# RMSNorm over 16,384 rows of 512: the order of the transfers, and the scaling spread over three engines

## The chip, the cores and the metric

The kernel runs on one core of a Trainium2 chip. The metric is the device time of one execution in microseconds (us); lower is better.

## The reference

```python
def reference(x, gamma):          # x: 16 x 1024 x 512 float32, gamma: 512 float32
    eps = 1e-5
    rms = np.sqrt(np.mean(x ** 2, axis=-1, keepdims=True) + eps)
    return (x / rms * gamma).astype(np.float32)
```

Each row of 512 numbers is divided by its own root mean square and multiplied, column by column, by `gamma`. 33.55 MB are read and as many written.

## The kernel before

The 16,384 rows are cut into four tiles (t = 0 to 3). A tile has 32 rows in each of the 128 partitions, so a partition's share of it is one run of 64 KB in the input, in SBUF and in the output. Three buffers, `slots[0]` to `slots[2]`, hold a tile each; the fourth tile goes into slot 0 again, once the first tile is stored (`slot_of`).

The computation is in place and goes by groups of 8 rows per partition. `row_stats` (L63) finds the rows' sums of squares in one of two ways, by turns. In one, ScalarE squares one row at a time and accumulates its sum itself (L76). In the other, ScalarE squares four rows into PSUM (L70) and VectorE sums them (L71). ScalarE then takes the root (L82) and VectorE the reciprocal, `rstd` (L83). `apply` (L86) multiplies each row by its `rstd` and by `gamma_b` (gamma copied to every partition) in one VectorE instruction (L88). The statistics of the next group are written ahead of the scaling of this one; Tile's scheduler sets the final order on each engine.

All large transfers are issued by the engine SP, on one queue, in the order of the program. `load` is L42, `store` L45. An instruction on SP that must wait holds up those behind it. Tile 0 comes in two loads; the others are issued by `transfers` (L100) after the group that they are tied to:

```python
if (t, g) == (0, 0):
    store(0, 0, 0, 1); load(1, 1, 0, 32); load(2, 2, 0, 16)
    store(0, 0, 1, 2); load(2, 2, 16, 32)
elif (t, g) == (0, 24): store(0, 0, 2, 32)
elif (t, g) == (1, 8):
    store(1, 1, 0, 16); load(3, 0, 0, 16); load(3, 0, 16, 32)
elif (t, g) == (1, 24): store(1, 1, 16, 32)
elif (t, g) == (2, 24): store(2, 2, 0, 32)
elif (t, g) == (3, 8):  store(3, 0, 0, 16)
elif (t, g) == (3, 24): store(3, 0, 16, 32)
```

The arguments are tile, slot, first row and row after the last. Below is the function with the line numbers that the profile uses.

Of the kernel before, what the change touches and what calls it, by code (L numbers as in the profile page):

```python
# [1 line left out]

# [4 lines left out]


@with_exitstack
def kernel(  # L10
    ctx: ExitStack,
    tc: tile.TileContext,
    x: bass.AP,
    gamma: bass.AP,
    out: bass.AP,
):
    nc = tc.nc
    P = nc.NUM_PARTITIONS
    eps = 1e-5
    fp32 = mybir.dt.float32  # L20
    AF = mybir.ActivationFunctionType
    OP = mybir.AluOpType

    xf = x.flatten_outer_dims()
    of = out.flatten_outer_dims()
    N, D = xf.shape
    R = 32
    G = 8
    H = 4
    assert N == 4 * P * R  # L30

    xv = xf.rearrange("(t p r) d -> t p r d", p=P, r=R)
    ov = of.rearrange("(t p r) d -> t p r d", p=P, r=R)

    const = ctx.enter_context(tc.tile_pool(name="const", bufs=1))
    stats = ctx.enter_context(tc.tile_pool(name="stats", bufs=4))
    psum = ctx.enter_context(tc.tile_pool(name="psum", bufs=2, space=bass.MemoryType.PSUM))

    slots = [const.tile([P, R, D], fp32, name=f"slot{i}") for i in range(3)]

    def load(t, slot, r0, r1):
        nc.sync.dma_start(out=slots[slot][:, r0:r1], in_=xv[t][:, r0:r1])  # L42

    def store(t, slot, r0, r1):
        nc.sync.dma_start(out=ov[t][:, r0:r1], in_=slots[slot][:, r0:r1])  # L45

    load(0, 0, 0, 8)
    load(0, 0, 8, 32)

    gamma_row = const.tile([1, D], fp32)  # L50
    nc.scalar.dma_start(out=gamma_row, in_=gamma.unsqueeze(0))
    ones_col = const.tile([1, P], fp32)
    nc.vector.memset(ones_col, 1.0)  # L53
    gamma_psum = psum.tile([P, H, D], fp32, name="sq")
    nc.tensor.matmul(gamma_psum[:, 0], ones_col, gamma_row, start=True, stop=True)  # L55
    gamma_b = const.tile([P, D], fp32)
    nc.vector.tensor_copy(out=gamma_b, in_=gamma_psum[:, 0])  # L57

    eps_t = const.tile([P, 1], fp32)
    nc.vector.memset(eps_t, eps)  # L60
    sq_scratch = const.tile([P, D], fp32)

    def row_stats(slot, g):  # L63
        ss = stats.tile([P, G], fp32, name="ss")
        rms = stats.tile([P, G], fp32, name="rms")
        rstd = stats.tile([P, G], fp32, name="rstd")
        if (g // G) % 2:
            for h in range(0, G, H):
                sq = psum.tile([P, H, D], fp32, name="sq")
                nc.scalar.activation(out=sq, in_=slots[slot][:, g + h : g + h + H, :], func=AF.Square)  # L70
                nc.vector.tensor_reduce(  # L71
                    out=ss[:, h : h + H], in_=sq, axis=mybir.AxisListType.X, op=OP.add
                )
        else:
            for r in range(G):
                nc.scalar.activation(  # L76
                    out=sq_scratch,
                    in_=slots[slot][:, g + r, :],
                    func=AF.Square,
                    accum_out=ss[:, r : r + 1],  # L80
                )
        nc.scalar.activation(out=rms, in_=ss, func=AF.Sqrt, bias=eps_t, scale=1.0 / D)  # L82
        nc.vector.reciprocal(out=rstd, in_=rms)  # L83
        return rstd

    def apply(slot, g, rstd):  # L86
        for r in range(G):
            nc.vector.scalar_tensor_tensor(  # L88
                out=slots[slot][:, g + r, :],
                in0=slots[slot][:, g + r, :],  # L90
                scalar=rstd[:, r : r + 1],
                in1=gamma_b,
                op0=OP.mult,
                op1=OP.mult,
            )

    groups = [(t, g) for t in range(4) for g in range(0, R, G)]
    slot_of = [0, 1, 2, 0]

    def transfers(t, g):  # L100
        if (t, g) == (0, 0):
            store(0, 0, 0, 1)
            load(1, 1, 0, 32)
            load(2, 2, 0, 16)
            store(0, 0, 1, 2)
            load(2, 2, 16, 32)
        elif (t, g) == (0, 24):
            store(0, 0, 2, 32)
        elif (t, g) == (1, 8):
            store(1, 1, 0, 16)  # L110
            load(3, 0, 0, 16)
            load(3, 0, 16, 32)
        elif (t, g) == (1, 24):
            store(1, 1, 16, 32)
        elif (t, g) == (2, 24):
            store(2, 2, 0, 32)
        elif (t, g) == (3, 8):
            store(3, 0, 0, 16)
        elif (t, g) == (3, 24):
            store(3, 0, 16, 32)  # L120

    ahead = row_stats(0, 0)
    for k, (t, g) in enumerate(groups):
        rstd = ahead
        if k + 1 < len(groups):
            tn, gn = groups[k + 1]
            ahead = row_stats(slot_of[tn], gn)
        apply(slot_of[t], g, rstd)
        transfers(t, g)


# [1 line left out]
_INS = ['x', 'gamma']  # L133
_OUTS = [((16, 1024, 512), 'float32')]


# [23 lines left out]
```

## Time and profile before

| | |
|---|---|
| median of 14 runs | 162.2 us (161.78 to 163.03) |
| profiled execution | 161.77 us |
| its span | 160.0 us |
| VectorE (DVE) busy | 122.6 us, 77% |
| ScalarE (ACT) busy | 80.1 us, 50% |
| GpSimd (POOL) busy | 0.2 us |
| moved | 67.13 MB, mean 420 GB/s |

A row of groups names line, engine, operation, output and inputs with their shapes and count; after the first bar stand the busy time in us and the mean ns of one instruction, after the second the engine's idle time just before these instructions and what ended it. In the row of DMA slices each digit is the busy share of a fortieth of the span in tenths. A row of waits names who waited for whom, the total in us, how many times, and the longest. "DMA" is the group of 16 transfer engines, "SPq" the queue that issues on SP.

### The profile page before, as it was taken

How to read it: one execution, taken by the hardware profiler on the slowest of the kernel's cores; microseconds unless marked ns; L12 is line 12 of the kernel's file. 1: busy time of each engine (PE TensorE's matmuls, PEld its weight loads, DVE VectorE, ACT ScalarE, POOL GpSimd, SP SyncE). 2: the span in 40 equal slices, each digit the busy share in tenths (PEclk: the TensorE clock that was granted, in tenths of full speed). 3: DMA queues.
4: the chain of work that ended last, by engine and by line, in shares of the span. 5: the costliest groups of instructions: out<-in, count | busy, mean ns of one | idle time of the engine just before them, and what ended most of it. 6: DMA issues, size and time to landing. Idle time of an engine off the chain costs nothing.

```text
span 160.0 us, 409 instructions
## 1 busy us (share of the span) xinstructions
PE 2.0 (1%) x2; PEld 0.5 (0%) x2; DVE 122.6 (77%) x163; ACT 80.1 (50%) x162; POOL 0.2 (0%) x4
## 2 busy tenths in 40 slices
PE   4000000000000000000000000000000000000000
PEld 1000000000000000000000000000000000000000
DVE  0101928999999509999999999999999999996000
ACT  3098029991291999996900960069709950000000
POOL 0000000000000000000000000000000000000000
DMA  5999999699699999997999999999997996999993
GB/s 197 524 393 393 406 512 524 262 524 492 295 395 400 452 500 401 494 476 338 415 393 475 434 401 451 451 410 426 467 516 311 508 492 295 467 434 410 451 442 156
DMA packets 2164, 67.13 MB, mean 420 GB/s; under 512 B 241, under 2 KB 241, under 8 KB 498
## 3 DMA queue, kind: packets, MB, share of 16 engines
q1 hardware_dynamic: 2160, 67.11, 97.8%
q14 instruction: 2, 0.02, 0.0%
q10 hardware_dynamic: 2, 0.00, 0.0%
HBM read 33.56 MB, written 33.55 MB: 419 GB/s over the span
## 4 chain that ended last, share of the span: by engine, by line
DVE 67%; DMA 14%; ACT 7%; issue 2%; DVEq 0%; SPq 0%
DVE slot L88 48%; DVE ss L71 18%; DMA slot<-in_x_dram 14%; ACT sq_scratch L76 3%; ACT sq L70 3%; DVE rstd L83 1%; ACT rms L82 1%; DVEq L155 0%; SPq L42 0%
## 5 line engine op out<-in xcount | busy, mean ns | idle before, releaser
L88 DVE SCALAR_TENSOR_TENSOR slot<-slot,rstd,gamma_b 128x512 f32<-128x512 f32 x128 | 85.8, 741 | 0.1
L76 ACT ACTIVATE sq_scratch<-slot 128x512 f32<-128x512 f32 x64 | 40.0, 625 | 9.9 <-DMA slot<-in_x_dram 8.6
L70 ACT ACTIVATE sq<-slot 128x2048 f32<-128x2048 f32 x16 | 29.8, 1865 | 18.9 <-DVE ss L71 11.5
L71 DVE TENSOR_REDUCE ss<-sq 128x4 f32<-128x2048 f32 x16 | 35.9, 2277 | 3.6 <-ACT sq L70 3.6
L82 ACT ACTIVATE rms<-ss,eps_t 128x8 f32<-128x8 f32 x16 | 4.6, 297 | 26.2 <-DVE ss L71 26.0
L83 DVE RECIPROCAL rstd<-rms 128x8 f32<-128x8 f32 x16 | 3.1, 196 | 16.2 <-ACT rms L82 16.2
L76 ACT ACTIVATION_READ_ACCUMULATOR sq_scratch<-slot 128x1 f32 x64 | 11.9, 187 | 0.0
L57 DVE COPY gamma_b<-sq 128x512 f32<-128x512 f32 x1 | 0.7, 692 | 3.2 <-PE sq L55 3.2
L55 PE MATMUL sq<-gamma_row,ones_col 1*128 1x512 f32 x2 | 2.0, 1122 | 2.1 <-DMA gamma_row<-in_gamma_dram 2.1
L76 ACT ACT_TABLE_LOAD x1 | 1.3, 1283 | 1.3 <-PEq L144 1.3
L82 ACT ACT_TABLE_LOAD x1 | 1.3, 1283 | 0.0
L53 DVE MEMSET ones_col<- 1x128 f32 x1 | 0.2, 165 | 0.8 <-PEq L144 0.8
L55 PEld LDWEIGHTS sq<-gamma_row,ones_col 1*128 1x128 f32 x2 | 0.5, 308 | 2.1 <-issue 2.1
L144 POOL MEMSET const-bfloat16-1.0<- 128x1 bf16 x1 | 0.1, 101 | 0.0
L144 POOL MEMSET const-uint8-127<- 128x1 uint8 x1 | 0.1, 101 | 0.0
L144 POOL MEMSET const-float32-0.0<- 128x1 f32 x1 | 0.1, 98 | 0.2 <-issue 0.2
L144 POOL MEMSET const-float32-1.0<- 128x1 f32 x1 | 0.1, 98 | 0.0
L60 DVE MEMSET eps_t<- 128x1 f32 x1 | 0.1, 59 | 0.0
## 6 DMA issues: line engine op xcount, KB each, us to landing
slot<-in_x_dram SPq DMA_DIRECT2D x4, 4096.0 KB, 32.1
out_dram<-slot SPq DMA_DIRECT2D x4, 4096.0 KB, 18.3
out_dram<-slot SPq DMA_DIRECT2D x1, 7680.0 KB
slot<-in_x_dram SPq DMA_DIRECT2D x1, 6144.0 KB, 21.7
slot<-in_x_dram SPq DMA_DIRECT2D x1, 2048.0 KB, 7.1
out_dram<-slot SPq DMA_DIRECT2D x2, 256.0 KB, 21.3
gamma_row<-in_gamma_dram ACTq DMA_DIRECT2D x1, 2.0 KB
slot<-in_x_dram SPq DMA_DIRECT2D x1, 25.9
```

The lines of the kernel that those rows point to most:

```text
L53: nc.vector.memset(ones_col, 1.0)
L55: nc.tensor.matmul(gamma_psum[:, 0], ones_col, gamma_row, start=True, stop=True)
L57: nc.vector.tensor_copy(out=gamma_b, in_=gamma_psum[:, 0])
L60: nc.vector.memset(eps_t, eps)
L70: nc.scalar.activation(out=sq, in_=slots[slot][:, g + h : g + h + H, :], func=AF.Square)
L71: nc.vector.tensor_reduce(out=ss[:, h : h + H], in_=sq, axis=mybir.AxisListType.X, op=OP.add)
L76: nc.scalar.activation(out=sq_scratch, in_=slots[slot][:, g + r, :], func=AF.Square, accum_out=ss[:, r : r + 1],)
L82: nc.scalar.activation(out=rms, in_=ss, func=AF.Sqrt, bias=eps_t, scale=1.0 / D)
L83: nc.vector.reciprocal(out=rstd, in_=rms)
L88: nc.vector.scalar_tensor_tensor(out=slots[slot][:, g + r, :], in0=slots[slot][:, g + r, :], scalar=rstd[:, r : r + 1], in1=gamma_b, op0=O ...
L144: nc = _bacc.Bacc("TRN2", target_bir_lowering=False, num_devices=1)
```

## The change

The transfers are in another order. The first tile comes in three loads, the second tile's load is issued ahead of the first store, and the last tile's two loads stand between the first tile's store and the second tile's. That store is one transfer of 64 KB rows. The engine order is now the program's own (`manual_schedule`).

The groups have 8 rows twice and then 16 rows. All sums of squares go the second way: ScalarE squares 7, 5 and 4 rows (4 and 4 in the small groups) into PSUM or SBUF by turns, VectorE sums them. Of each group's rows, the last 3, 7 or 8 (the last number of a group's entry) are scaled on GpSimd, in two instructions: by `rstd`, then by gamma. The others are scaled by `rstd` one row at a time on ScalarE and by gamma in bulk on VectorE, in halves where the group has 16 rows. `declare_no_dep` takes from the bulk multiply those waits for transfers and GpSimd work on the same rows that ScalarE has had already. Gamma is fetched in six pieces, and its copy to all partitions is made by ScalarE.

```diff
     load(0, 0, 0, 8)
-    load(0, 0, 8, 32)
+    load(0, 0, 8, 16)
+    load(0, 0, 16, 32)
+    load(1, 1, 0, 32)
...
+    groups = [
+        (0, 0, 8, (4, 4), 3),
+        (0, 8, 8, (4, 4), 3),
+        (0, 16, 16, (7, 5, 4), 7),
+        (1, 0, 16, (7, 5, 4), 8),
+        (1, 16, 16, (7, 5, 4), 8),
+        (2, 0, 16, (7, 5, 4), 8),
+        (2, 16, 16, (7, 5, 4), 7),
+        (3, 0, 16, (7, 5, 4), 7),
+        (3, 16, 16, (7, 5, 4), 3),
+    ]
...
+    def square_sums(ss, t, g, r, m, k):
+        home, name, most = ((psum, "sq_psum", 7), (const, "sq_sbuf", 5))[k % 2]
+        sq = home.tile([P, most, D], fp32, name=name)
+        rows = slots[slot_of[t]][:, g + r : g + r + m, :]
+        nc.scalar.activation(out=sq[:, :m], in_=rows, func=AF.Square)
+        nc.vector.tensor_reduce(
+            out=ss[:, r : r + m, 0], in_=sq[:, :m], axis=mybir.AxisListType.X, op=OP.add
+        )
...
+    def scale_by_pool(rstd, t, g, n, share):
+        part = slots[slot_of[t]][:, g + n - share : g + n, :]
+        by_row = rstd[:, n - share : n].to_broadcast([P, share, D])
+        nc.gpsimd.tensor_tensor(out=part, in0=part, in1=by_row, op=OP.mult)
+        last = nc.gpsimd.tensor_tensor(
+            out=part, in0=part, in1=gamma_b.to_broadcast([P, share, D]), op=OP.mult
+        )
...
+    def scale_rows(rstd, t, g, r0, r1):
+        x = slots[slot_of[t]]
+        for r in range(r0, r1):
+            nc.scalar.activation(out=x[:, g + r, :], in_=x[:, g + r, :], func=AF.Copy, scale=rstd[:, r])
+        part = x[:, g + r0 : g + r1, :]
+        scaled = nc.vector.tensor_tensor(out=part, in0=part, in1=gamma_b.to_broadcast([P, r1 - r0, D]), op=OP.mult)
+        for slot, b0, b1, earlier in before_scale:
+            if slot == slot_of[t] and b0 < g + r1 and g + r0 < b1:
+                tc.declare_no_dep(scaled.ins, earlier.ins, reason="ScalarE waited for it before it scaled these rows")
 
     def transfers(t, g):
         if (t, g) == (0, 0):
             store(0, 0, 0, 1)
-            load(1, 1, 0, 32)
             load(2, 2, 0, 16)
             store(0, 0, 1, 2)
-            load(2, 2, 16, 32)
-        elif (t, g) == (0, 24):
-            store(0, 0, 2, 32)
-        elif (t, g) == (1, 8):
-            store(1, 1, 0, 16)
+            load(2, 2, 16, 24)
+            store(0, 0, 2, 3)
+            load(2, 2, 24, 32)
+        elif (t, g) == (0, 16):
+            store(0, 0, 3, 16)
+            store(0, 0, 16, 32)
             load(3, 0, 0, 16)
             load(3, 0, 16, 32)
-        elif (t, g) == (1, 24):
-            store(1, 1, 16, 32)
-        elif (t, g) == (2, 24):
+        elif (t, g) == (1, 16):
+            store(1, 1, 0, 32)
+        elif (t, g) == (2, 16):
             store(2, 2, 0, 32)
-        elif (t, g) == (3, 8):
+        elif (t, g) == (3, 0):
             store(3, 0, 0, 16)
-        elif (t, g) == (3, 24):
+        elif (t, g) == (3, 16):
             store(3, 0, 16, 32)
...
+    for k, group in enumerate(groups):
+        t, g, n, pieces, share = group
+        mine = n - share
+        half = (mine + 1) // 2
+        ahead = groups[k + 1 :][:1]
+        ss, todo = pieces_of(ahead[0]) if ahead else (None, [])
+        scale_by_pool(rstd, t, g, n, share)
+        for piece in todo[:2]:
+            square_sums(*piece)
+        if n < 16:
+            scale_rows(rstd, t, g, 0, mine)
+        else:
+            scale_rows(rstd, t, g, 0, half)
+        for piece in todo[2:]:
+            square_sums(*piece)
+        if n == 16:
+            scale_rows(rstd, t, g, half, mine)
         transfers(t, g)
+        for nxt in ahead:
+            rstd = inverse_rms(ss, nxt[2])
```

## The prediction, made before the changed kernel ran

> **What bounds the kernel now.** I read the page's row of DMA slices and its queue table first, because reading and writing 32 MiB each way is most of the work; then the groups, then the waits of the queue SP, then VectorE's timeline round the one store that comes nearest to being late.
>
> ```profile
> DMA  5999999699699999997999999999997996999993
> ...
> q1 hardware_dynamic: 2160, 67.11, 97.8%
> ```
>
> The transfer engines are full from the second slice to the last but one, and SP's queue fills 97.8% of their span. The trace's packet records say the same without rounding: the first load packet starts 1.74 us into the span, the last store packet ends at 158.8, and no engine of the 16 is without a packet between. A 64 KB packet took 2.418 us; a tile (32 rows of 2 KB in each of 128 partitions) is 8 such packets per engine, **19.34 us**. Eight tile transfers (four in, four out) are 154.8 of the 157.1 us. So the compute engines matter only where a store comes too late to keep the stream going.
>
> ```profile
> L88 DVE SCALAR_TENSOR_TENSOR slot<-slot,rstd,gamma_b 128x512 f32<-128x512 f32 x128 | 85.8, 741 | 0.1
> L76 ACT ACTIVATE sq_scratch<-slot 128x512 f32<-128x512 f32 x64 | 40.0, 625 | 9.9 <-DMA slot<-in_x_dram 8.6
> L70 ACT ACTIVATE sq<-slot 128x2048 f32<-128x2048 f32 x16 | 29.8, 1865 | 18.9 <-DVE ss L71 11.5
> L71 DVE TENSOR_REDUCE ss<-sq 128x4 f32<-128x2048 f32 x16 | 35.9, 2277 | 3.6 <-ACT sq L70 3.6
> ```
>
> These are the prices: 741 ns to scale a row, 625 for a row's ScalarE pass, 1865 for squares and 2277 for sums of four rows. GpSimd has none of the work. The queue's own waits:
>
> ```profile
> SPq L45 <- DVE slot L88: 120.5, 7, 29.8
> SPq L155 <- DMA out_dram<-slot: 12.0, 2, 9.6
> SPq L45 <- DMA slot<-in_x_dram: 10.3, 2, 6.3
> SPq L42 <- DMA out_dram<-slot: 8.4, 1, 8.4
> ```
>
> SP stands 120.5 us behind VectorE, and it costs nothing: each store is issued while earlier transfers still run. How near it comes is seen on VectorE:
>
> ```profile
> 105.94 9.97 DVE L88 SCALAR_TENSOR_TENSOR slot<-slot,rstd,gamma_b 128x512 f32<-128x512 f32 x15
> 115.84 4.48 DVE L71 TENSOR_REDUCE ss<-sq 128x4 f32<-128x2048 f32 x2
> ```
>
> The 15 rows end tile 2 at 115.9; the packet records show the sixth tile transfer done at **119.1**, and tile 2's store is the seventh. The cover is 3.2 us, of which about 1.0 is issue (the first load is issued at 0.73 and its first packet starts at 1.74).
>
> **What the Trainium skill says.** "GPSIMD Engine Reference", 3.1 Elementwise: an fp32 `tensor_tensor` of 2048 elements took 4497 ns there, 2.196 ns an element, since both inputs come through one read port; no run here shows it yet. "SBUF — State Buffer", Who interferes with whom: a VectorE instruction with two SBUF inputs contends with a GpSimd instruction that reads SBUF, and the second to start waits for the first to end; a `tensor_reduce` never contends. The trace before has no GpSimd work to show either. "VectorE: DVE Perf Modes", the TRN2 errata section: fp32 `tensor_tensor` is (N+151)/0.96 ns, 2291 for 2048; the sums' 2277 for as many elements agrees. Prices from "ScalarE: Activation LUTs", What ACT_TABLE_LOAD costs: 186 + 0.833 N ns, 93 more for a pointer operand and about 93 of overlap back to back; 1892 for 2048 against 1865 in the trace.
>
> **The change part by part.**
>
> *Transfers.* The bytes are the same. Tile 1's store goes from 16 packets per engine of 32 KB (1217 ns mean) to 8 of 64 KB: 16 x 1.217 - 8 x 2.418 = 0.1 us less. The first tile's rest goes as 16 and 32 KB rows instead of 48 KB rows, which took 1867 ns where 48/64 of 2418 is 1814: at most 8 x 53 ns = 0.4 us. Three small stores instead of two and the six gamma pieces lie under loads. The load of tile 1 is issued ahead of the first store, so it no longer stands behind VectorE on SP, but the stream had been covered to 22.1 anyway: nothing. The last tile's two loads wait on SP for tile 0's stores, with half-tile transfers (9.7 us) running meanwhile, and tile 1's store stands behind them: nothing while rows are ready. I take 0 for all, with -0.5 to +0.3 as ends.
>
> *ScalarE and VectorE.* Before, a row costs VectorE 741 ns and a part of the sums. After, all 128 rows are squared to a buffer (7, 5 and 4 rows: 3.15, 2.3, 1.87 us) and summed on VectorE (3.9, 2.8, 2.3); 74 rows are scaled on ScalarE (0.61 each) and multiplied by gamma on VectorE in pieces of 4 or 5 rows (2.3 or 2.8). A group of 16 rows: VectorE 9.0 + 4.6 + 0.1 = 13.7, ScalarE 7.3 + 4.9 + 0.3 = 12.5. Since the square of the next group waits for the root, VectorE idles about 1 us: a period of **14.7 us**. These engines are in step with the loads up to tile 1: it lands at 42.1 (22.8 as in the chain before, and 19.3). From there: square 3.2, sums of 7 and 5 rows 6.7, tile 0's last 5 rows 2.8, sum of 4 rows 2.3, 4 rows 2.3: 59.4. Then the first `rstd` of tile 1 is out. Three more periods and one of 15.2 put VectorE's part of tile 2 at about 118.5. Plus 1.0 to issue this is 119.5, against 119.1: just at the edge.
>
> *GpSimd.* It takes 3+3+7+8+8+8+7+7+3 = 54 rows, two instructions each. 8 rows are 2 x 4096 x 2.196 = 18.0 us, 7 rows 15.7, 3 rows 6.7. Tile 0's shares are done early (the third group's at about 54). From 59.4: 77.4, 95.4 (tile 1), 113.4, **129.1** (tile 2), 144.8, 151.5 (tile 3). Tile 1's store is wanted at 99.8: covered. Tile 2's can start at 130.1 where the stream runs dry at 119.1: **11.0 us idle**. It then runs to 149.4, and tile 3's halves (144.8; 151.5 against 159.1) follow without a gap. What was hidden by 3.2 us of cover is uncovered, and no later transfer wins it back.
>
> *Waits taken away.* `declare_no_dep` spares VectorE's multiply the waits for earlier DMAs; ScalarE has waited for them. Nothing moves by it: VectorE waits for ScalarE's last row.
>
> Sum: the profiled execution took 161.77 us (span 160.0, 1.77 around it), 0.4 below the median 162.2. 161.8 + 11.0 = 172.8; against the median **173.2**.
>
> **Bounds of the unknown.** GpSimd's element: the instruction has two reads through a port at 1.2 GHz, so 1.67 ns at the least by the page; at 1.85 ns (58.7 us for the 62 row passes between 59.4 and 118.1) it is hidden. Blocking adds from nothing to all of VectorE's multiplies.
>
> **Rivals.** *The stream stays full* (for: only 15% has to be missing from a price that no run here has shown; the queue was covered before; against: the page's figure, VectorE itself at the edge). Then only the transfers' terms remain: 161.4 to 162.7, at 161.9. This is the case that ends not slower; it decides below 1.85 ns an element and with multiplies that are not held up. *The two engines exclude each other* (for: page and shapes, every multiply has `slot` and `gamma_b` in SBUF; against: the page measured no such pair in this mix). Between 59.4 and tile 2's end VectorE multiplies 33 rows, 18.9 us: tile 1 comes 5.8 us late (95.4 + 9.2 + 1.0 against 99.8), tile 2 at 149.0 against 124.9, tile 3's halves at 169.8 against 168.3 and at 183.8 against 179.5: 5.8 + 24.1 + 1.5 + 4.3 = 35.7, so about 198. *The change does not do what it says*: little room, since the built order on SP has both loads of tile 3 ahead of tile 1's store.
>
> **How the numbers follow.** Late by GpSimd's pace, with some of the blocking at most: 0.45, 165 to 187, at 173.2. Exclusion in full: 0.22, about 187 to 200. Full stream: 0.33, at 161.9. Differences under 0.2% (0.3 us) can hardly be told from none. Of the full stream's 0.33, 0.17 is faster by more than that, 0.11 the same and 0.05 slower; the others are slower: 0.72. The range, 161.3 to 191, leaves out most of the exclusion (0.13) and little below; the likeliest case alone has 165 to 187.
>
> **What would show it.** Right: GpSimd near 9 us for 128x4096 and busy without a gap from 60 to 150 us; SP's longest wait for tile 2's store ends on GpSimd; one dip of the DMA row near three quarters of the span, and none else. Multiplies on VectorE of 128x2048 that last far over 2.3 us, or start late behind GpSimd, would show exclusion. Wrong: a DMA row without a dip, with GpSimd's 4096 below 7.6 us.

## The result, and the profile after

The changed kernel takes **206.45 us** (median of 10 runs, 205.58 to 206.68) against 162.09 us before: 1.272 times as long, 95% interval 1.271 to 1.274. The profiled execution has a span of 204.3 us, 44.3 more than before. The forecast was 173.2 us with a range to 191; slower was right, the size was not.

First the row of DMA slices and the queue table of the page after:

```profile
DMA  7999999999899999999400999900000999499297
...
q1 hardware_dynamic: 2592, 67.11, 76.9%
```

The stream was full before; now it has two large holes and ends ragged. The packet records give them their size: no engine has a packet from 100.35 to 114.34 us (tile 1's store is late), from 133.9 to 158.36 (tile 2's), and for 1.7 and 3.6 us ahead of tile 3's halves. That is 14.0 + 24.5 + 1.7 + 3.6 = 43.8 of the 44.3 us.

Next, the groups, with different shapes kept apart (same form: busy us and mean ns after the first bar, idle time ahead after the second):

```profile
L111 ACT ACTIVATE slot<-slot,ss 128x512 f32<-128x512 f32 x74 | 46.7, 706 | 2.1 <-DVE ss L96 2.1
L113 DVE TENSOR_TENSOR slot<-slot,gamma_b 128x2048 f32<-128x2048 f32 x9 | 45.3, 5031 | 0.0
...
L90 DVE TENSOR_REDUCE ss<-sq_psum 128x7 f32<-128x3584 f32 x7 | 27.2, 3891 | 8.4 <-ACT sq_psum L89 8.4
L103 POOL TENSOR_TENSOR slot<-slot,gamma_b 128x4096 f32<-128x4096 f32 x3 | 26.4, 8814 | 0.2
...
L102 POOL TENSOR_TENSOR slot<-slot,ss 128x4096 f32<-128x4096 f32 x3 | 21.0, 7016 | 20.9 <-DVE ss L96 20.9
```

ScalarE and the sums cost what was worked out. VectorE's multiply of 2048 elements has a mean of 5.0 us where 2.3 was reckoned, and that mean hides the point, since it lies between instructions of 2.3 and of 10.5 us, as the timeline of one group shows (start us, duration us, engine, line, operation; between brackets the idle time ahead and what ended it):

```profile
68.27 7.02 POOL L102 TENSOR_TENSOR slot<-slot,ss 128x4096 f32<-128x4096 f32 x1 [7.32 <-DVE ss L96]
...
69.25 3.89 DVE L90 TENSOR_REDUCE ss<-sq_psum 128x7 f32<-128x3584 f32 x1 [1.06 <-ACT sq_psum L89]
...
73.06 2.81 DVE L90 TENSOR_REDUCE ss<-sq_sbuf 128x5 f32<-128x2560 f32 x1
...
75.36 8.81 POOL L103 TENSOR_TENSOR slot<-slot,gamma_b 128x4096 f32<-128x4096 f32 x1
...
75.78 10.54 DVE L113 TENSOR_TENSOR slot<-slot,gamma_b 128x2048 f32<-128x2048 f32 x1
86.25 2.28 DVE L90 TENSOR_REDUCE ss<-sq_psum 128x4 f32<-128x2048 f32 x1
88.45 2.28 DVE L113 TENSOR_TENSOR slot<-slot,gamma_b 128x2048 f32<-128x2048 f32 x1
...
90.65 0.24 DVE L96 RECIPROCAL ss<-ss 128x16 f32<-128x16 f32 x1
90.97 7.02 POOL L102 TENSOR_TENSOR slot<-slot,ss 128x4096 f32<-128x4096 f32 x1 [6.79 <-DVE ss L96]
```

The sums at 69 and 73 run at full speed beside GpSimd. The multiply at 75.78 comes while GpSimd is in its second pass (75.36 to 84.17) and ends at 86.32: 2.15 us after that pass. A free multiply of this size takes 2.28 us, so this one stood still for some 8.3 us. The third sum, the second multiply and the reciprocal stand behind it, and GpSimd, which needs that reciprocal, then has nothing to do for 6.8 us. So a group is a chain: 7.0 + 8.8 us on GpSimd, then 2.15 + 2.2 + 2.2 + 0.2 on VectorE, with the hand-overs **22.7 us**. The queue SP waits for VectorE as before, but now the stream runs dry while it does; the first of these rows has the two longest waits, ahead of the stores of tiles 1 and 2:

```profile
SPq L49 <- DVE slot L113: 139.4, 6, 43.5
SPq L49 <- DVE ss L96: 25.5, 1, 25.5
SPq L45 <- DMA out_dram<-slot: 12.8, 2, 9.8
```

And the beginning, from the timeline of the first 17 us:

```profile
1.18 3.97 ACTq L60 DMA_DIRECT2D gamma_row<-in_gamma_dram  x6
...
13.98 2.04 PE L64 MATMUL sq_psum<-gamma_row,ones_col 1*128 1x512 f32 x2 [13.98 <-DMA gamma_row<-in_gamma_dram]
16.06 0.59 ACT L66 COPY gamma_b<-sq_psum 128x512 f32<-128x512 f32 x1 [9.60 <-PE sq_psum L64]
16.68 1.88 ACT L89 ACTIVATE sq_psum<-slot 128x2048 f32<-128x2048 f32 x1
```

The same places in the timeline of before:

```profile
2.15 2.04 PE L55 MATMUL sq<-gamma_row,ones_col 1*128 1x512 f32 x2 [2.15 <-DMA gamma_row<-in_gamma_dram]
...
7.86 0.63 ACT L76 ACTIVATE sq_scratch<-slot 128x512 f32<-128x512 f32 x1 [5.31 <-DMA slot<-in_x_dram]
```

Before, the matmul (it copies gamma to all partitions) got gamma at 2.15 us and the first square started at 7.86, when its rows had landed. Now the six pieces have landed only at 13.9, ScalarE's copy of gamma waits for the matmul, and the first square stands behind that copy in ScalarE's queue: it starts 8.8 us later. Not every execution loses as much here: seven of the ten lie between 206.37 and 206.68 us, three between 205.58 and 205.79, and all six-piece variants profiled below had gamma at 12.9 to 13.2 us, not 14.0. So about 1 us of any difference to 206.45 can be due to when gamma happened to land.

### The profile page after: what moved, and what is told of

Same layout as the page of the kernel before. It is cut to its first block, busy times and chain, and to the rows that moved or that the text cites. A ratio compares the mean times of both kernels' runs of the same rounds, so it can differ in the third digit from the quotient of the medians.

```text
span 204.3 us, 288 instructions
## 1 busy us (share of the span) xinstructions
PE 2.0 (1%) x2; PEld 0.5 (0%) x2; DVE 156.8 (77%) x50; ACT 108.2 (53%) x111; POOL 108.2 (53%) x24
## 4 chain that ended last, share of the span: by engine, by line
DVE 66%; ACT 18%; DMA 4%; ACTq 2%; DVEq 2%; PE 1%; issue 1%
DVE slot L113 33%; DVE ss L90 32%; ACT sq_psum L89 12%; DMA gamma_row<-in_gamma_dram 4%; ACT slot L111 3%; ACTq L60 2%; DVEq L199 2%; PE sq_psum L64 1%; ACT sq_sbuf L89 1%; ACT ss L95 1%; ACT L95 1%; ACTq L199 0%; ACT gamma_b L66 0%; DVE ss L96 0%; ACTq L34 0%
## 5 line engine op out<-in xcount | busy, mean ns | idle before, releaser
L113 DVE TENSOR_TENSOR slot<-slot,gamma_b 128x2048 f32<-128x2048 f32 (+3 forms) x16 | 85.6, 5352 | 4.9 <-ACT slot L111 4.9
L102 POOL TENSOR_TENSOR slot<-slot,ss 128x1536 f32<-128x1536 f32 (+2 forms) x9 | 47.8, 5308 | 75.8 <-DVE ss L96 75.8
L90 DVE TENSOR_REDUCE ss<-sq_psum 128x4 f32<-128x2048 f32 (+1 forms) x16 | 47.8, 2985 | 28.6 <-ACT sq_psum L89 28.6
L103 POOL TENSOR_TENSOR slot<-slot,gamma_b 128x1536 f32<-128x1536 f32 (+2 forms) x9 | 60.0, 6669 | 0.7
L111 ACT ACTIVATE slot<-slot,ss 128x512 f32<-128x512 f32 x74 | 46.7, 706 | 2.1 <-DVE ss L96 2.1
L89 ACT ACTIVATE sq_psum<-slot 128x2048 f32<-128x2048 f32 (+1 forms) x16 | 38.7, 2421 | 0.0
L95 ACT ACTIVATE ss<-ss,eps_t 128x16 f32<-128x16 f32 (+1 forms) x9 | 2.7, 304 | 59.1 <-DVE ss L90 59.1
L90 DVE TENSOR_REDUCE ss<-sq_sbuf 128x5 f32<-128x2560 f32 (+1 forms) x9 | 24.2, 2690 | 0.0
L89 ACT ACTIVATE sq_sbuf<-slot 128x2560 f32<-128x2560 f32 (+1 forms) x9 | 20.0, 2226 | 0.0
L96 DVE RECIPROCAL ss<-ss 128x16 f32<-128x16 f32 (+1 forms) x9 | 2.1, 231 | 2.1 <-ACT ss L95 2.1
```

Source lines behind the costliest of these rows:

```text
L89: nc.scalar.activation(out=sq[:, :m], in_=rows, func=AF.Square)
L90: nc.vector.tensor_reduce(out=ss[:, r : r + m, 0], in_=sq[:, :m], axis=mybir.AxisListType.X, op=OP.add)
L95: nc.scalar.activation(out=ss[:, :n, 0], in_=ss[:, :n, 0], func=AF.Sqrt, bias=eps_t, scale=1.0 / D)
L96: nc.vector.reciprocal(out=ss[:, :n, 0], in_=ss[:, :n, 0])
L102: nc.gpsimd.tensor_tensor(out=part, in0=part, in1=by_row, op=OP.mult)
L103: last = nc.gpsimd.tensor_tensor(out=part, in0=part, in1=gamma_b.to_broadcast([P, share, D]), op=OP.mult)
```

## Experiments

Two theories of the loss had to be told apart, and each from its rivals. **Exclusion**: a VectorE instruction with two SBUF inputs can't run while a GpSimd instruction reads SBUF. **Gamma late**: the start is lost to the six small transfers. Where an expectation speaks of "the port", it means what the two engines would share under the first theory. Unless said otherwise, an edit is against the changed kernel.

### Gamma in one piece

```diff
-    pieces = (0, 96, 176, 256, 336, 416, D)
+    pieces = (0, D)
```

> The changed kernel with gamma fetched in one transfer instead of six. Theory A (VectorE's multiply and GpSimd exclude each other, and the late gamma is a second cost of its own): gamma lands near 7.4 us instead of 13.9, the first square starts near 10 instead of 16.7, the groups behind tile 1's landing start some 6 us earlier, and every later store with them: about 200 us. Rival B (the late start is absorbed by the loads, which gate the groups at 42 us anyway): 205 to 206.5. The multiply on VectorE stays near 10.5 us in both.

Measured: **200.76 us**. From its timeline:

```profile
7.86 2.04 PE L64 MATMUL sq_psum<-gamma_row,ones_col 1*128 1x512 f32 x2 [7.86 <-DMA gamma_row<-in_gamma_dram]
9.94 0.59 ACT L66 COPY gamma_b<-sq_psum 128x512 f32<-128x512 f32 x1 [4.74 <-PE sq_psum L64]
10.56 1.88 ACT L89 ACTIVATE sq_psum<-slot 128x2048 f32<-128x2048 f32 x1
```

Gamma lands 6.1 us earlier, and 5.7 us of that reach the end. The loads absorb only part of it: the first sum of tile 1, which needs tile 1 loaded, starts 3.9 us earlier (45.80 us for 49.66). But the multiply behind that tile's first two sums waits for GpSimd's pass over tile 0's last rows, which owes nothing to that load and ends 6.1 us earlier (54.85 for 60.94). In the changed kernel's packet records each gamma piece is one packet of data and one of 4 bytes, probably for its semaphore, and nearly all of these twelve start some 0.62 us after the one before: the time of one 16 KB packet of the loads (0.61). It looks as if they take turns with the loads, a packet each, so that six pieces wait some twelve times where one waits twice; no run was made to test this.

### VectorE's gamma in PSUM

```diff
-    gamma_psum = psum.tile([P, 7, D], fp32, name="sq_psum")
+    gamma_psum = psum.tile([P, 1, D], fp32, name="gamma_psum")
...
-        scaled = nc.vector.tensor_tensor(out=part, in0=part, in1=gamma_b.to_broadcast([P, r1 - r0, D]), op=OP.mult)
+        scaled = nc.vector.tensor_tensor(out=part, in0=part, in1=gamma_psum.to_broadcast([P, r1 - r0, D]), op=OP.mult)
```

> The changed kernel, but VectorE's bulk multiply takes gamma from a PSUM copy instead of SBUF, so it has one SBUF input; GpSimd still takes the SBUF copy, and nothing else moves. Theory A (the second SBUF input is what shuts VectorE out while GpSimd works): the multiplies of 2048 elements fall from up to 10.5 us to about 2.3, GpSimd works nearly without gaps at 15.9 us for 8 rows, tile 2's store can start near 126 us against a dry stream at 119: about 169 us. Rival C (VectorE is slowed by something else: the shape of the multiply, or both engines on the same rows of a slot): multiplies stay near 10 us and the time above 200.

Measured: **167.49 us**, 39.0 less than the changed kernel, for the place of one operand. Its timeline, for the same part of a group as above:

```profile
62.54 7.01 POOL L102 TENSOR_TENSOR slot<-slot,ss 128x4096 f32<-128x4096 f32 x1 [2.67 <-DVE ss L96]
...
69.63 8.87 POOL L103 TENSOR_TENSOR slot<-slot,gamma_b 128x4096 f32<-128x4096 f32 x1
...
70.06 2.28 DVE L113 TENSOR_TENSOR slot<-slot,gamma_psum 128x2048 f32<-128x2048 f32 x1
...
74.45 2.28 DVE L113 TENSOR_TENSOR slot<-slot,gamma_psum 128x2048 f32<-128x2048 f32 x1
...
78.45 7.02 POOL L102 TENSOR_TENSOR slot<-slot,ss 128x4096 f32<-128x4096 f32 x1
```

The same multiply, at the same place beside GpSimd's second pass, takes 2.28 us. GpSimd's passes keep their length, and the next follows without a gap. Both engines still work on rows of the same slot, so that is not what held the multiply up. VectorE's period is 14.4 us. Gamma landed 1.0 us earlier than in the profile of the changed kernel, so up to about 1 us of the 39.0 may not be the operand's.

### Without GpSimd

```diff
-        mine = n - share
+        mine = n
...
-        scale_by_pool(rstd, t, g, n, share)
```

> The changed kernel with GpSimd's share of the rows given to ScalarE and VectorE (all 16 rows of a group scaled there, GpSimd scales none). Theory A: the multiplies of 4096 elements take 4.4 us each and never more, a group takes VectorE 9.0 + 8.9 + 1.3 = 19.2 us instead of 22.7, and the time falls to about 191 us although VectorE has 54 rows more. Rival D (GpSimd's help is worth what it takes off VectorE, and the loss is elsewhere, in the order of the transfers or in ScalarE's row scaling): above 206.

Measured: **188.17 us**. The multiplies are as expected:

```profile
L113 DVE TENSOR_TENSOR slot<-slot,gamma_b 128x4096 f32<-128x4096 f32 x16 | 70.8, 4423 | 8.5 <-ACT slot L111 8.4
```

With 54 more rows on ScalarE and VectorE the kernel is 18.3 us faster: in the changed form GpSimd's help costs more than it brings.

### The order of the transfers alone

On the kernel before, with only the changed list of loads and stores:

```diff
-    load(0, 0, 8, 32)
+    load(0, 0, 8, 16)
+    load(0, 0, 16, 32)
+    load(1, 1, 0, 32)
...
-            store(1, 1, 0, 16)
             load(3, 0, 0, 16)
             load(3, 0, 16, 32)
...
-            store(1, 1, 16, 32)
+            store(1, 1, 0, 32)
```

> The kernel before with only the transfers in the changed order (three loads for tile 0, the last tile's loads before tile 1's store, that store whole); its computation is kept. Theory A (the order by itself costs and brings nothing, since the stream stays full): 161.7 to 162.4 us, DMA row full. Rival D (the order starves the stream): some us above 163, with a dip in the DMA row after tile 3's loads.

Measured: **162.44 us** against 162.06, ratio 1.0022 (1.0013 to 1.0031). The row of slices has no hole:

```profile
DMA  6999999969799999999999999799799799699992
```

By the packet records an engine has 157.05 us of packets instead of 156.54. The 0.5 us are not the price of more and smaller packets: in the load of tile 1 one packet of each engine, started between 38.7 and 39.1 us, took 2.93 to 3.09 us where the others of 64 KB took 2.42, which is 0.6 us. The profile of before has a similar slow packet on every engine at 20.0 to 20.3 us, of 2.02 to 2.37 us for 1.82. What slows them is open. The order starves nothing and brings nothing.

### Both repairs

The edits of the first two experiments together.

> Both repairs in one: VectorE's gamma from PSUM, and gamma fetched in one transfer; shares and order as changed. Theory A, with the prices now measured (GpSimd 15.9 us for 8 rows, 13.9 for 7, without gaps once VectorE is not shut out): the first root of tile 1 comes at about 59.7, tile 2's GpSimd rows end at 59.7 + 3 x 15.9 + 13.9 = 121.3, its store starts near 122.3 against a dry stream at 119.2: about 3 us idle, 164.5 to 165. Rival (the two costs are one and the same, so that the second repair adds nothing): 167.5.

Measured: **164.82 us**. The packet records have one hole, 119.8 to 122.3, ahead of tile 2's store, whose last GpSimd pass ends at 121.45. So with exclusion gone the forecast's own mechanism, GpSimd's pace, is what is left, at 2.5 us.

### Both repairs, an earlier start, a smaller share

```diff
-    nc.scalar.addr_align(128, offset=0, max_nops=0)
...
-    load(1, 1, 0, 32)
+    load(1, 1, 0, 16)
+    load(1, 1, 16, 32)
...
-        (2, 0, 16, (7, 5, 4), 8),
+        (2, 0, 16, (7, 5, 4), 7),
```

with the edits of both repairs.

> Both repairs, and three further edits that are to take the rest of the idle time away: tile 1 comes in two loads, so that its first group can start before 42 us; GpSimd has 7 rows of the group (2, 0) instead of 8; the instruction-alignment call is left out, which may let gamma be issued before the first load. Theory A: tile 2 is ready near 117, before the stream runs dry at 119, so there is no idle time: 161.7 to 162.4, the same as before within 0.3%. Rival (some other wait shows once GpSimd's is gone, at tile 3's end, say): 163 to 165.

Measured: **162.89 us** against 162.19, ratio 1.0039 (1.0025 to 1.0054). The stream is full again:

```profile
DMA  5999999999999999999999999899899899899993
```

The time is still 0.7 us over that of before and above what I expected. The medians of the spans differ by 0.3 us only (160.7 against 160.4), about the extra packet time (156.93 against 156.54 in the profiles). The other 0.4 us lie outside the span: device time less span is 2.14 to 2.23 us in these runs and 1.73 to 1.82 before. That part comes up again in "All waits kept".

Without the alignment call gamma is issued at 0.73 us instead of 1.16 and its packet starts at 1.64 instead of 6.69, ahead of the loads' packets. The first square then starts at 7.96, when its rows have landed, where one piece alone had brought it to 10.56 only. So the late start had a second cause beside the pieces: gamma's place behind the first loads. The three further edits were not tried one by one. With no idle time left to win, work spread over three engines has nothing to give here.

### GpSimd without the gamma tile

GpSimd's second pass gets the operand of its first, so that its rows are not multiplied by gamma.

```diff
         last = nc.gpsimd.tensor_tensor(
-            out=part, in0=part, in1=gamma_b.to_broadcast([P, share, D]), op=OP.mult
+            out=part, in0=part, in1=by_row, op=OP.mult
         )
```

> The changed kernel, but GpSimd's second pass multiplies by the reciprocal root again instead of gamma; gamma is left out of GpSimd's rows. GpSimd then reads no byte of the gamma tile that VectorE reads. Theory A (it is any GpSimd instruction with SBUF inputs that shuts out VectorE's second input): VectorE's long multiplies still wait for GpSimd's second pass, which is shorter (7.0 us instead of 8.8), so they last about 8.7 us and the time is 194 to 197. Rival E (both engines reading the one gamma tile is the conflict): multiplies of 2.3 us, about 169 or less.

Measured: **194.77 us**. From the timelines of GpSimd and VectorE:

```profile
72.89 7.02 POOL L103 TENSOR_TENSOR slot<-slot,ss 128x4096 f32<-128x4096 f32 x1
...
73.32 8.74 DVE L113 TENSOR_TENSOR slot<-slot,gamma_b 128x2048 f32<-128x2048 f32 x1
```

The long multiplies last 8.74 us and still end 2.15 us after GpSimd's pass. It is not the shared gamma tile: a pass that reads only the slot and the reciprocal root does it too, for as long as it lasts.

### The third sum ahead of the multiply

```diff
-        for piece in todo[:2]:
+        for piece in todo:
             square_sums(*piece)
...
-        for piece in todo[2:]:
-            square_sums(*piece)
```

> The changed kernel with the third square and sum of the next group written ahead of the first multiply, so that on VectorE it no longer stands behind the multiply that waits for GpSimd. Theory A (a group is a serial chain: GpSimd's two passes, then what VectorE has still to do before the next reciprocal): the chain of a 16-row group falls from 22.7 to about 20.5 us, six times, so about 193 us. Rival F (the period is set by the sum of VectorE's own work): no change, 206.

Measured: **192.19 us**. The group's period is 20.5 us (GpSimd's first passes start at 64.86, 85.39 and 105.92), 2.2 us less: the time of the sum that was moved. So what stands behind the blocked multiply on VectorE is part of the chain.

### The reciprocal ahead of the multiplies, too

The edit of the experiment before, and:

```diff
+        coming = [inverse_rms(ss, nxt[2]) for nxt in ahead]
         if n < 16:
             scale_rows(rstd, t, g, 0, mine)
...
-        for nxt in ahead:
-            rstd = inverse_rms(ss, nxt[2])
+        for nxt in coming:
+            rstd = nxt
```

> The changed kernel with the next group's three sums, its root and its reciprocal all ahead of this group's multiplies. GpSimd then has the next group's work at hand while VectorE's multiplies wait, so it is seen who gets the port. Theory A1 (it passes, at the end of a GpSimd instruction, to VectorE if that waits): multiplies wait for the rest of one GpSimd instruction, at most 8.8 us, GpSimd shows gaps of about 2.2 us in front of an instruction, a 16-row group takes 15.9 + 4.4 = 20.3 us or a little more, 187 to 193 us in all. Theory A2 (GpSimd keeps it while it has an instruction queued): single multiplies last 20 us and more, GpSimd runs two groups without a gap, and the time is near 206 or above.

Measured: **244.04 us**; my time was far off. From its timeline:

```profile
94.47 7.01 POOL L102 TENSOR_TENSOR slot<-slot,ss 128x4096 f32<-128x4096 f32 x1 [11.58 <-DVE ss L96]
96.59 17.86 DVE L113 TENSOR_TENSOR slot<-slot,gamma_b 128x2048 f32<-128x2048 f32 x2 [2.20 <-ACT slot L111]
...
101.57 10.73 POOL L103 TENSOR_TENSOR slot<-slot,gamma_b 128x4096 f32<-128x4096 f32 x1
114.38 3.88 DVE L90 TENSOR_REDUCE ss<-sq_psum 128x7 f32<-128x3584 f32 x1
```

The turn does pass at the end of an instruction, and in both directions: the first multiply gets in between GpSimd's passes (7.01 us end at 101.48), and now GpSimd's second pass waits for it, 10.73 us instead of 8.81. But the second multiply waits for that whole pass, to 112.3, and ends at 114.4. I had not seen that an earlier reciprocal sends GpSimd into the next group ahead of this group's multiplies, so that both of them are caught and the sums of the group after stand behind them: 29.4 us a group.

### All waits kept

Without the loop over `before_scale` that calls `declare_no_dep`.

> The changed kernel without declare_no_dep: the multiplies on VectorE wait for every earlier transfer and GpSimd instruction on their rows. Theory A: these waits are over when ScalarE has scaled the rows, so the time stays within 0.3 us of 206.4. Rival: a wait for a transfer shows ahead of a multiply, and the time rises by 1 us or more.

Measured: **205.03 us**, outside the 0.3 us, and faster. The multiplies are the same (5032 ns mean for 2048 elements against 5031), and no wait for a transfer shows ahead of one. Two things differ. The matmul waits for gamma to 12.9 us instead of 14.0, and all that follows is earlier by 1.0 to 1.1 us. That is not shown to be the edit's doing: every other profiled variant with six pieces keeps `declare_no_dep` and has gamma at 12.9 to 13.2 as well, and three of the changed kernel's own executions are some 0.8 us shorter than the rest.

The other 0.4 us lie outside the span. Device time less span is 1.76 to 1.80 us in the four runs here, as in the runs of the kernel before and of its two variants (1.73 to 1.84). In the changed kernel and in every variant that keeps `declare_no_dep` it is 2.14 us or more. So leaving these calls out saves 0.4 us there, and the waits that they remove cost nothing; why they lengthen the time outside the span is open.

### GpSimd in instructions of two rows

```diff
-        nc.gpsimd.tensor_tensor(out=part, in0=part, in1=by_row, op=OP.mult)
+        cuts = [(a, min(a + 2, share)) for a in range(0, share, 2)]
+        for a, b in cuts:
+            nc.gpsimd.tensor_tensor(out=part[:, a:b], in0=part[:, a:b], in1=rstd[:, n - share + a : n - share + b].to_broadcast([P, b - a, D]), op=OP.mult)
```

and the second pass likewise.

> The changed kernel with GpSimd's two passes cut into instructions of two rows (8 rows: 4 + 4 instructions of 1.75 and 2.2 us). Theory A1 (the port is held for one instruction and then given to VectorE if it waits): a multiply of 2048 elements waits 2.2 us at most and lasts up to 4.5 us instead of 10.5; GpSimd's passes then grow by VectorE's 4.4 us, and a 16-row group takes 20.5 to 21 us: about 195 us. Theory A2 (GpSimd keeps the port through back-to-back instructions): multiplies stay near 10.5 us and the time near 206, or above by what 30 more instructions cost.

Measured: **199.12 us**, between the two figures but with the first theory's marks. From the groups that keep shapes apart:

```profile
L105 POOL TENSOR_TENSOR slot<-slot,gamma_b 128x1024 f32<-128x1024 f32 x24 | 71.2, 2992 | 0.0
...
L115 DVE TENSOR_TENSOR slot<-slot,gamma_b 128x2048 f32<-128x2048 f32 x9 | 25.8, 2865 | 0.0
```

The multiply falls from a mean of 5.0 us to 2.9, and GpSimd's two-row pass is 2.99 us where a quarter of 8.81 would be 2.20. Short instructions make VectorE's wait short and GpSimd's passes longer. How much of the longer passes is waiting, and how much the price of more instructions, was not separated.

### Fewer, larger transfers

On the kernel before:

```diff
     load(0, 0, 8, 32)
+    load(1, 1, 0, 32)
+    load(2, 2, 0, 32)
...
-            store(0, 0, 2, 32)
+            store(0, 0, 0, 32)
...
-            load(3, 0, 0, 16)
-            load(3, 0, 16, 32)
+            load(3, 0, 0, 32)
```

and without the two small stores and the loads that stood between them.

> The opposite of the changed order, on the computation of before: fewer and larger transfers. Tile 2 and tile 3 are loaded whole, tile 0 is stored whole, the two small stores are gone, and the loads of tiles 1 and 2 are issued at the start. Theory A (with a full stream only the packets' own times count; the trace of before has 156.5 us of packet time per engine, of which 154.8 is the share of 64 KB packets): 48 packets of 32 KB per engine go as 24 of 64 KB, 0.2 to 0.4 us less, the small stores 0.1, so 161.5 to 161.9 against 162.1 for before. Rival (a tile that lands whole comes too late for VectorE, and a store is late): 163 or more, with a dip in the DMA row.

Measured: **165.35 us**. The rival was right: tile 3 lands whole at 110.0 us instead of its first half at 90, VectorE ends at 151.4 instead of 146.6, and the last store is late. The packet records have a hole of 2.0 us ahead of that store. Tile 2's load also took 20.6 us instead of 19.3, all of it in one packet of each engine, started between 58.0 and 58.7 us, which took 3.4 to 3.9 us instead of 2.42; the cause is open. The two make up nearly all of the 3.4 us over before. The split loads of the kernel before earn their packets. No version tried here beats it.

## Why the prediction was wrong

**The bound, and where a loss would show: right.** Before, the stream was all but full (an engine's packets fill 156.54 of 157.1 us). Only late stores cost, and the idle stream is the loss (43.8 of 44.3 us). But the one hole that was forecast, at tile 2's store, is one of four: tile 1's store, held to be covered, came 14.0 us late, before tile 2's.

**The price of VectorE's multiply: the step that failed.** The forecast took 2.3 us for 2048 elements and gave exclusion a chance of 0.22, because no trace and no measured pair had shown the two engines together. With GpSimd in its pass it took 10.5. The Trainium skill had said it: "SBUF — State Buffer", Who interferes with whom, has a two-input VectorE instruction contend with a GpSimd instruction that reads SBUF, and the second to start wait. Every multiply of the change has two SBUF inputs and every GpSimd pass reads SBUF. The runs agree: whole instructions wait, sums don't, one input in PSUM frees it. Every GpSimd pass here writes SBUF too, so that the reads are what counts is shown by no run. The cost by itself is 206.45 - 167.49 = **39.0 us**, of which about 1 us may be gamma's landing. A rule that fits the shapes of the change exactly should have been the likeliest case, not the rival.

**The exclusion rival: mechanism right, time 198 for 206.45.** Its period of 18.0 + 4.6 = 22.6 us met the measured 22.7 by luck. GpSimd's passes are 15.9, not 18.0; but what stands behind the blocked multiply, 2.2 of sum and 0.2 of reciprocal, is in series as well. The rival let GpSimd run on. Its start, 59.4 us for the first root of tile 1 where GpSimd started on that tile at 68.27, left out gamma (6.1 us, to 62.17 with one piece) and the first blocked multiply (2.5 more, to 59.72 with both repairs).

**GpSimd's pace: right in kind, mis-sized.** 2.196 ns an element was taken from "GPSIMD Engine Reference", 3.1 Elementwise. Measured are 1.71 for the pass by `rstd` (7.02 us for 4096) and 2.15 for the pass by gamma (8.81), 1.93 together. The starts of passes that follow without a gap, 7.09 and 8.82 us apart, say the same. With both repairs that left 2.5 us of idle stream, not 11.0.

**Gamma in six pieces "under loads": wrong.** The step asked only whether the transfer engines had room. It did not ask who waits for gamma: ScalarE's copy, ahead of its first square. It cost 5.7 us by itself (206.45 - 200.76), 2.7 once exclusion is gone (167.49 - 164.82).

**The order of the transfers at 0, -0.5 to +0.3: nearly right.** It measures +0.4 us. The 0.4 us that it hoped to win on rows of 48 KB were not there: these took 1.815 us in the run with larger packets, the share of a 64 KB packet, and the 1.867 before was mostly the slow packet at 20 us. **`declare_no_dep` at nothing:** right for the waits, and 0.4 us too low for the time outside the span. **VectorE's period of 14.7 and ScalarE's prices:** 14.4 once nothing blocks, and 3.16 us for five scaled rows where 5 x 0.61 = 3.05 was reckoned.

In sum: 206.45 - 39.0 (exclusion) - 2.7 (gamma) - 1.9 (the three further edits) = 162.9. The 0.7 us that this is above the kernel before are 0.3 of span, about the extra packet time, and 0.4 outside the span.

## What to carry to other kernels

Before giving GpSimd part of VectorE's work, look at what both read: here a VectorE multiply with two SBUF inputs waited for the whole GpSimd pass beside it (10.5 us for 2.3), and everything behind it on VectorE waited as well; one input in PSUM removed the wait. Price a blocked instruction by its queue, not by itself. A small transfer can land late behind large ones (13.9 us here in six pieces, 7.9 in one, 2.6 issued ahead of the loads), so ask who stands behind it. And in a kernel whose transfers are never idle ask first what faster arithmetic could bring.

## What was not expected of the hardware

GpSimd's multiply by one number per row, spread over 512 elements, takes 1.71 ns an element; by a row of gamma, 2.15. The exclusion goes both ways: a GpSimd pass that comes second is held too (10.73 us for 8.81). VectorE's sums, from PSUM or SBUF, left GpSimd's passes as they were (7.02 us beside two sums, 7.01 without one). In several profiles one packet on each of the 16 transfer engines is slow at the same moment, by 0.3 to 1.3 us in the mean (20 us into the profile of before, 39 in that of the order alone, 58 in that of the larger transfers).
